# Whole banks gathered before their readout, and a gate unit moved from the first pair of experts to the last

## The chip, the cores and the metric

The kernel runs on one core of a Trainium2 chip. The metric is the device time of one execution in microseconds, the median of the runs shown; a profiled execution gives the trace.

## What is computed

Two blocks of a language model run one after the other on 512 tokens of 1024 features, in float32. The change touches the mixture of experts that ends each of the two layers of the second block:

```
def expert_choice_moe(x, router_w, w1, w3, w2):
    cap = EC_CAPACITY_FACTOR * s // N_EXPERTS
    aff = jax.nn.softmax(jnp.einsum('bsd,de->bse', x, router_w).astype(jnp.float32), axis=-1)
    gates, idx = lax.top_k(aff.transpose(0, 2, 1), cap)
    xg = jax.vmap(lambda xb, ib: xb[ib])(x, idx)
    hid = jax.nn.silu(jnp.einsum('becd,edf->becf', xg, w1)) * jnp.einsum('becd,edf->becf', xg, w3)
    ye = jnp.einsum('becf,efd->becd', hid, w2) * gates[..., None].astype(x.dtype)
    return jax.vmap(lambda yb, ib: jnp.zeros((s, d), x.dtype).at[ib.reshape(-1)].add(yb.reshape(-1, d)))(ye, idx)
...
        ffn = expert_choice_moe(x, router_w[i], w1[i], w3[i], w2[i])
        ple = jax.nn.sigmoid(x @ ple_gate_w[i] + ple_gate_b[i]) * (p[i] @ ple_w[i])
        x = layer_norm(DEEPNORM_ALPHA * x + ffn + ple, ln2_g[i], ln2_b[i])
```

There are 16 experts, each takes 64 of the 512 tokens, and w1, w3 and w2 of an expert are 1024x1024 each. `ple` is a gated side input; its 1024 features are worked out in eight units of 128.

## The kernel before

`experts` (called by `moe`, once in each layer: the first and the second stage below) goes through eight pairs of experts, `pi` 0 to 7. The weights of a pair are 24 chunks of 128x2048 floats (1024 KB). SyncE issues all their loads in one order, into a ring of eight buffers (`cyc`: three of the pool `wr`, five of `r1`); a load waits until the chunk eight places before it has been used. A unit's gate weights (`unit`, 512 KB) take one place in the same ring, and its second weights `pw` (128x256) have a buffer of their own.

A pair runs like this. For each half of the hidden features, `pair_product` multiplies w1 into `a1` and w3 into `a3`, eight chunks a half: two experts side by side, 64 columns each, the chunks as the moving operand. Between the first half and the second TensorE scatters the result of the pair before (`scatter`, `sc`), works out a unit if the table `units_a` names one, and transposes the selection `og` (`ot`). After the second half it finishes an open unit (`rest`, the transposes `pt`), turns the hidden values (`hidden`, `ht`), gathers the tokens of the next two pairs if `pi` is 1, 3 or 5 (`gather`), works out a unit if `units_b` names one, and multiplies w2 (`y`, eight chunks). Units 0 and 1 of the eight are worked out before the stage. For pair 0 the gather is split: two banks before the first product, two between the products of w1 and w3 with the first and the second half of the inputs (`kc`).

`gather` makes the 1024 features of the chosen tokens, eight tiles of 128x256, two tiles to a bank of PSUM: eight matmuls a tile with the one-hot matrix `OH`, then a scale and shift into `xg`, on VectorE for the bank's first tile and on ScalarE for its second (L1664 to L1671). `ple_unit` splits the gate weights into a high part (`whi`, ScalarE, L218) and a low part (`wlo`, VectorE or every fourth time GpSimd, L221), does 24 matmuls into `pg` and 6 into `pv`, and takes tanh of `pg`.

TensorE's order in `experts` is kept as it is written (`keep_order`); the other engines and SyncE follow a scheduler. At the last pair `ef.close()` gives back the memory that the units use, and in the second layer the gain and bias of the final norm (`lng`, `lnb`, 512 KB each) are loaded into it.

Of the kernel before, what the change touches and what calls it, by code (L numbers as in the profile page):

```python
# [14 lines left out]
AF = mybir.ActivationFunctionType  # L15
OP = mybir.AluOpType
# [129 lines left out]
class K:  # L146
# [1473 lines left out]
    def experts(self, l, xhl, aff, slT, slot, g, b, st, ef, r1, early):  # L1620
        nc, I, C = self.nc, self.ins, self.C
        x = self.xtok
        w1, w3, w2 = I["w1_2"][l], I["w3_2"][l], I["w2_2"][l]
        with ExitStack() as es:
# [25 lines left out]
            def one_hot(grp):  # L1650
                OH = p.tile([128, 4, 4, 64], F32R, name="OH")
                nc.vector.tensor_tensor(OH, slT[:, :, 4 * grp:4 * grp + 4, None].to_broadcast([128, 4, 4, 64]),
                                        slot[:, None, None, :].to_broadcast([128, 4, 4, 64]), op=OP.is_equal)
                return OH

            def gather(xg, OH, k2s):

                for k2 in k2s:
                    ps = pp.tile([128, 2, 256], F32, name="ga", tag=("t", "y", "sc", "y")[k2])
                    for kk in range(2):  # L1660
                        k = 2 * k2 + kk
                        for t in range(4):
                            for a in range(2):
                                nc.tensor.matmul(ps[:, kk], xhl[a][:, t, 128 * k:128 * k + 128],  # L1664
                                                 OH[:, t].rearrange("p e s -> p (e s)"),
                                                 start=t == 0 and a == 0, stop=t == 3 and a == 1)
                        if kk:
                            nc.scalar.activation(xg[:, k], ps[:, kk], AF.Identity, scale=g[:, k:k + 1], bias=b[:, k:k + 1])
                        else:
                            nc.vector.tensor_scalar(xg[:, k], ps[:, kk], g[:, k:k + 1], b[:, k:k + 1],  # L1670
                                                    op0=OP.mult, op1=OP.add)  # L1671

            def hidden(th, half, hT):
                ps = pp.tile([128, 4, 128], F32, name="ht", tag="t")
# [4 lines left out]
            def scatter(oT, ys, halves, last=False):  # L1679
                for half in halves:  # L1680
                    yh, yl = ys[half]
                    for t in range(4):
                        ps = pp.tile([128, T], F32, name="sc", tag=("y", "sc")[t % 2] if not last else "sc")
                        ts_ = slice(128 * t, 128 * t + 128)
                        nc.tensor.matmul(ps, oT[:, ts_], yh, start=True, stop=False)  # L1685
                        nc.tensor.matmul(ps, oT[:, ts_], yl, start=False, stop=True)  # L1686
                        xs = x[:, t, 512 * half:512 * half + 512]
                        nc.vector.tensor_add(xs, xs, ps)  # L1688
                        if last:
                            self.ln_stats(p, st[:, t], x[:, t], half)  # L1690
                            if half and l == 0:
                                self.ln_norm(p, st[:, t], x[:, t])
# [9 lines left out]
            def rest(u):  # L1702
                if u:
                    next(u)

            first = len(nc.cur_bb.bb.instructions)
            OH = one_hot(0)
            xg = p.tile([128, 8, 256], F32, name="xg")
            gather(xg, OH, range(2))
            left = u = None  # L1710
            units_a, units_b = {0: 2, 3: 5}, {0: 3, 2: 4, 4: 6, 6: 7}
            for pi in range(8):
                grp, pr = divmod(pi, 2)
                e0 = 2 * pi

                og = p.tile([128, 4, 2, 64], F32, name="og")
                nc.gpsimd.tensor_mul(og, OH[:, :, 2 * pr:2 * pr + 2], aff[:, :, e0:e0 + 2, None].to_broadcast([128, 4, 2, 64]))  # L1717
                if pr and pi < 7:
                    OH = one_hot(grp + 1)
                hT = p.tile([128, 8, 128], F32, name="hT")  # L1720
                ths = []
                for half in range(2):
                    xa = lambda a, k: xg[:, k, 128 * pr + 64 * a:128 * pr + 64 * a + 64]
                    a1, a3 = [pp.tile([128, T], F32, name="a", tag="a") for _ in range(2)]
                    for kc in range(2):
                        if pi == half == 0 and kc == 1:
                            gather(xg, OH, range(2, 4))
                        pair_product(a1, w1, e0, xa, half, kc)
                        if pi == half == kc == 0:
                            for h in range(2):  # L1730
                                G, Bb = self.ln_half(p, l, h, "yh", "yl")
                                for t in range(4):
                                    xs = x[:, t, 512 * h:512 * h + 512]
                                    nc.gpsimd.tensor_mul(xs, xs, G)
                                    nc.gpsimd.tensor_add(xs, xs, Bb)
                                for m in range(2) if h == 0 else ():
                                    xs = x[:, :, 128 * m:128 * m + 128]
                                    nc.gpsimd.tensor_add(xs, xs, early[m].rearrange("p (t f) -> p t f", t=4))
                        pair_product(a3, w3, e0, xa, half, kc)
                    th = p.tile([128, T], F32, name="th", bufs=2)  # L1740
                    nc.scalar.activation(th, a1, AF.Tanh, scale=0.5)  # L1741
                    nc.vector.scalar_tensor_tensor(th, th, 1.0, a1, op0=OP.add, op1=OP.mult)  # L1742
                    nc.vector.tensor_mul(th, th, a3)
                    ths.append(th)

                    rest(u)
                    u = None
                    if half == 0:
                        if left:
                            scatter(*left, range(2))  # L1750
                        if pi in units_a:
                            u = unit(units_a[pi])
                        ps = pp.tile([128, T], F32, name="ot", tag="t")
                        for t in range(4):
                            nc.tensor.transpose(ps[:, 128 * t:128 * t + 128], og[:, t].rearrange("p e s -> p (e s)"), C["ident"])
                        gate = p.tile([128, 1], F32, name="gate", bufs=2)
                        ogT = p.tile([128, T], F32, name="ogT", tag="og")
                        nc.scalar.activation(ogT, ps, AF.Copy, scale=0.5, accum_out=gate)
                        oT = p.tile([128, T], F32R, name="oT", bufs=2)
                        nc.vector.tensor_scalar(oT, ogT, 0.0, None, op0=OP.is_gt)  # L1760
                        if pi == 7:
                            ef.close()
                            if l == 1:
                                G, Bb = self.ln_load(es.enter_context(self.pool("lng", 1, side="right")), l, "ln2")
                    else:
                        hidden(ths[0], 0, hT)
                        if pr and pi < 7:
                            xg = p.tile([128, 8, 256], F32, name="xg")
                            gather(xg, OH, range(4))
                        if pi in units_b:  # L1770
                            u = unit(units_b[pi])
                        hidden(th, 1, hT)
                if pi == 7:
                    self.exp_ln_table()
                ys = []
                for half in range(2):
                    y = pp.tile([128, T], F32, name="y", tag="y")
                    for kc in range(2):
                        pair_product(y, w2, e0, lambda a, k: hT[:, k, 64 * a:64 * a + 64], half, kc)
                        if pi == 7 and half and kc == 0:  # L1780
                            scatter(oT, ys, range(1), True)
                    yh = p.tile([128, T], F32R, name="yh", bufs=2)
                    yl = p.tile([128, T], F32R, name="yl", bufs=2)
                    nc.scalar.activation(yh, y, AF.Copy, scale=gate)  # L1784
                    nc.vector.scalar_tensor_tensor(yl, y, gate, yh, op0=OP.mult, op1=OP.subtract)  # L1785
                    ys.append((yh, yl))
                left = oT, ys
            scatter(*left, range(1, 2), True)
            self.keep_order(first)
            if l == 1:  # L1790
# [111 lines left out]
```

## Time and profile before

| what | value |
| --- | --- |
| three runs, median (lowest to highest) | 3506.03 us (3505.88 to 3511.51) |
| the profiled execution, its own time | 3509.84 us |
| its span, first to last instruction | 3508.0 us |
| mean granted TensorE clock | 0.971 |
| busy share of the span: PE, PEld, DVE, ACT, POOL | 94%, 61%, 45%, 31%, 15% |
| HBM over the span | 166 GB/s |

PE is TensorE's matmuls, PEld its weight loads, DVE is VectorE, ACT ScalarE, POOL GpSimd, SP SyncE. The busy share of an engine is a mean over stages that differ: the middle of a row of slices tells more than the share. A DMA share is the mean busy share of 16 DMA engines.

### The profile page before, as it was taken

What the parts mean: (1) busy time and instruction counts of PE and PEld (TensorE: products, weight loads), DVE (VectorE), ACT (ScalarE), POOL (GpSimd) and SP (SyncE); (2) the same over time, 40 slices, a digit from 0 to 9 for tenths busy, and PEclk for the clock granted to TensorE, in tenths of its full rate; (3) what the DMA queues carried; (4) which work ended last, traced back from release to release, by engine and by line L of the source; (5) the groups of instructions that cost most, each with busy time, mean ns of one, the idle gap of its engine ahead of it and who ended that gap; (6) DMA issues with size and microseconds to landing.
All of it is one profiled execution on the core that took longest, in us unless ns stands there. A gap on an engine that the chain in (4) does not pass through costs nothing. (4 is left out here: it accounts for less than half of the span.)

```text
span 3508.0 us, 37612 instructions
## 1 busy us (share of the span) xinstructions
PE 3305.6 (94%) x15018; PEld 2155.8 (61%) x15018; DVE 1582.8 (45%) x2527; ACT 1070.3 (31%) x1933; POOL 510.7 (15%) x357
## 2 busy tenths in 40 slices
PE   8999999999999999999989889999997999999996
PEld 6666578888766657888866765344435657444342
DVE  6555463444555546344457753122216775211213
ACT  4333333223333333322355432011013553111011
POOL 2012121001101212100230423000003103100001
PEclk9999999999999999999999989999998998999998
DMA  5101132234210113233220225999992013899997
GB/s 183 48 25 61 37 110 81 96 96 137 75 60 13 61 36 106 77 96 96 90 86 3 72 102 227 407 412 386 417 421 85 28 43 113 366 408 378 421 407 301
DMA packets 223583, 584.85 MB, mean 167 GB/s; under 512 B 17584, under 2 KB 160304, under 8 KB 173232
## 3 DMA queue, kind: packets, MB, share of 16 engines
q1 hardware_dynamic: 222976, 581.66, 43.9%
q8 instruction: 118, 1.93, 0.2%
q10 hardware_dynamic: 432, 0.79, 0.1%
q14 instruction: 57, 0.47, 0.0%
HBM read 580.30 MB, written 2.10 MB: 166 GB/s over the span
## 5 line engine op out<-in xcount | busy, mean ns | idle before, releaser
L218 ACT CAST whi<-w 128x1024 fp32r<-128x1024 f32 (+1 forms) x312 | 311.2, 1003 | 731.7 <-PE mm L228 498.8
L1647 PE MATMUL a<-w,xg 128*64 128x512 f32 x2048 | 481.4, 600 | 42.2 <-DMA w<-in_w_dram 42.2
L227 PE MATMUL mm<-h,whi 128*128 128x512 f32 x1056 | 417.9, 396 | 4.8 <-ACT whi L218 4.1
L229 PE MATMUL mm<-h,wlo 128*128 128x512 f32 x1056 | 415.0, 394 | 0.4 <-POOL wlo L221 0.3
L228 PE MATMUL mm<-l,whi 128*128 128x512 f32 x1056 | 412.0, 390 | 0.0
L221 DVE TENSOR_TENSOR wlo<-w,whi 128x1024 fp32r<-128x1024 f32 (+1 forms) x237 | 306.4, 1297 | 233.8 <-ACT whi L218 232.5
L1647 PEld LDWEIGHTS a<-w,xg 128*64 128x64 f32 x2048 | 158.5, 138 | 348.6 <-issue 252.8
L221 POOL TENSOR_TENSOR wlo<-w,whi 128x1024 fp32r<-128x1024 f32 x75 | 166.2, 2218 | 642.4 <-ACT whi L218 445.0
L1647 PE MATMUL y<-w,hT 128*64 128x512 f32 x1024 | 226.3, 594 | 3.3 <-DMA w<-in_w_dram 3.3
L227 PEld LDWEIGHTS mm<-h,whi 128*128 128x128 f32 x1056 | 199.3, 189 | 48.1 <-ACT whi L218 5.3
L229 PEld LDWEIGHTS mm<-h,wlo 128*128 128x128 f32 x1056 | 199.0, 188 | 47.2 <-DVE wlo L221 1.0
L228 PEld LDWEIGHTS mm<-l,whi 128*128 128x128 f32 x1056 | 199.0, 188 | 44.7 <-issue 0.7
L602 DVE TENSOR_REDUCE mx<-s 128x1 f32<-128x128 f32 x192 | 93.3, 489 | 192.6 <-PE s L601 191.7
L1742 DVE SCALAR_TENSOR_TENSOR th<-th,a 128x512 f32<-128x512 f32 x32 | 22.0, 688 | 317.5 <-ACT th L1741 317.5
L1647 PEld LDWEIGHTS y<-w,hT 128*64 128x64 f32 x1024 | 72.4, 137 | 144.8 <-issue 136.3
L604 ACT ACTIVATE P<-s,mx 128x128 f32<-128x128 f32 x192 | 100.9, 527 | 174.5 <-DVE mx L602 162.3
L948 POOL TENSOR_TENSOR u<-u 128x512 f32<-128x512 f32 x64 | 66.6, 1040 | 521.4 <-ACT E L947 275.5
L1717 POOL TENSOR_TENSOR og<-OH,aff 128x512 f32<-128x512 f32 x16 | 16.8, 1047 | 764.2 <-DVE oT L1760 747.6
L1785 DVE SCALAR_TENSOR_TENSOR yl<-y,gate,yh 128x512 fp32r<-128x512 f32 x32 | 24.0, 751 | 223.3 <-ACT yh L1784 223.3
L959 DVE TENSOR_TENSOR y<-mm,r 128x512 f32<-128x512 f32 x64 | 44.2, 691 | 160.8 <-PE mm L229 160.8
L1741 ACT ACTIVATE th<-a 128x512 f32<-128x512 f32 x32 | 19.1, 597 | 319.8 <-PE a L1647 319.8
L621 PEld LDWEIGHTS pt<-c_ident,P 128*128 128x128 f32 x480 | 54.8, 145 | 73.1 <-issue 63.9
(584 smaller groups left out, 6414.2 us busy)
## 6 DMA issues: line engine op xcount, KB each, us to landing
w<-in_w_dram SPq DMA_DIRECT2D x384, 1024.0 KB, 12.6
w<-in_w_in_dram SPq DMA_DIRECT2D x32, 1024.0 KB, 5.3
w<-in_w_up_dram SPq DMA_DIRECT2D x32, 1024.0 KB, 5.5
w<-in_w_down_dram SPq DMA_DIRECT2D x32, 1024.0 KB, 5.1
w<-in_w_out_dram SPq DMA_DIRECT2D x8, 1024.0 KB, 5.2
w<-in_w_o_dram SPq DMA_DIRECT2D x8, 1024.0 KB, 4.7
w<-in_ple_gate_w_dram SPq DMA_DIRECT2D x16, 512.0 KB, 4.9
w<-in_w_in_even_dram SPq DMA_DIRECT2D x7, 1024.0 KB, 5.4
```

The costliest lines, as they stand in the source:

```text
L218: nc.scalar.copy(h, view)
L221: e.tensor_sub(l, view, h)
L227: mm(ps, wh, xh, start=first, stop=False)
L228: mm(ps, wh, xl, start=False, stop=False)
L229: mm(ps, wl, xh, start=False, stop=last)
L602: nc.vector.tensor_reduce(mx[:, i:i + 1], s[:, :n], axis=X, op=OP.max, negate=True)
L604: nc.scalar.activation(pv, s[:, :n], AF.Exp, bias=mx[:, i:i + 1], accum_out=sums[:, i:i + 1])
L621: nc.tensor.transpose(ps[:, (i - k) * 128:(i - k + 1) * 128], P[h][0][i][:, k * 128:(k + 1) * 128], C["ident"])
L948: nc.gpsimd.tensor_mul(u, u, u)
L959: nc.vector.tensor_mul(y, ps, r2)
L1647: nc.tensor.matmul(ps[64 * a:64 * a + 64], lhs(a, 4 * kc + k), cw[a][:, k], start=kc == 0 and k == 0, stop=kc == 1 and k == 3)
L1785: nc.vector.scalar_tensor_tensor(yl, y, gate, yh, op0=OP.mult, op1=OP.subtract)
```

## The change

In `gather` both tiles of a bank are multiplied first, then read out, one by VectorE and one by ScalarE. The tables of the units change: pair 0 had units 2 and 3, pair 2 unit 4, pair 3 unit 5, pair 4 unit 6 and pair 6 unit 7; now pairs 0, 2, 3, 4, 6 and 7 have one each, 2 to 7 in order. Since pair 7 now has a unit, `ef.close()` and the load of the last norm's gain and bias come after the loop.

```
                         for t in range(4):
                             for a in range(2):
                                 nc.tensor.matmul(ps[:, kk], xhl[a][:, t, 128 * k:128 * k + 128], ...
-                        if kk:
-                            nc.scalar.activation(xg[:, k], ps[:, kk], AF.Identity, scale=g[:, k:k + 1], bias=b[:, k:k + 1])
-                        else:
-                            nc.vector.tensor_scalar(xg[:, k], ps[:, kk], g[:, k:k + 1], b[:, k:k + 1],
-                                                    op0=OP.mult, op1=OP.add)
+                    k = 2 * k2
+                    nc.vector.tensor_scalar(xg[:, k], ps[:, 0], g[:, k:k + 1], b[:, k:k + 1], op0=OP.mult, op1=OP.add)
+                    nc.scalar.activation(xg[:, k + 1], ps[:, 1], AF.Identity, scale=g[:, k + 1:k + 2], bias=b[:, k + 1:k + 2])
...
-            units_a, units_b = {0: 2, 3: 5}, {0: 3, 2: 4, 4: 6, 6: 7}
+            units_a, units_b = {3: 4, 7: 7}, {0: 2, 2: 3, 4: 5, 6: 6}
...
-                        if pi == 7:
-                            ef.close()
-                            if l == 1:
-                                G, Bb = self.ln_load(es.enter_context(self.pool("lng", 1, side="right")), l, "ln2")
...
                 left = oT, ys
+            ef.close()
+            if l == 1:
+                G, Bb = self.ln_load(es.enter_context(self.pool("lng", 1, side="right")), l, "ln2")
             scatter(*left, range(1, 2), True)
```

On ScalarE, in pair 0 of a stage, before: `xg<-ga` are the readouts of the gather's second tiles, `whi` is the split of unit 2's gate weights.

```order
L1668 ACTIVATE xg<-ga,cols 128x256 [waits DVE_49,PE_49] x2
L218 CAST whi<-w 128x1024 [waits DMAHW0_49,Activation_49]
L1668 ACTIVATE xg<-ga,cols 128x256 [waits DVE_49,PE_49] x2
L1741 ACTIVATE th<-a 128x512 [waits PE_49]
L1607 ACTIVATE pz<-pg,cols 128x512 [waits PE_49,Pool_49]
```

The same place now:

```order
L1669 ACTIVATE xg<-ga,cols 128x256 [waits DVE_49] x4
L1739 ACTIVATE th<-a 128x512 [waits PE_49]
L1756 ACTIVATE ogT,gate<-ot 128x512 [waits PE_49,Pool_49]
L1739 ACTIVATE th<-a 128x512 [waits PE_49]
L218 CAST whi<-w 128x1024 [waits DMAHW0_49,Activation_49]
```

The split of unit 2 stands behind all four readouts and both halves' tanh, and a readout waits for VectorE alone, whose own waits for TensorE. VectorE's `wlo` moved in the same way.

On TensorE, after the second gather of pair 0 (`ga`) and the products that follow it, what was added ahead of the unit's matmuls (`pg`) there:

```order
 L1664 MATMUL ga<-OH,xkl 128x256
 L1647 MATMUL a<-w,xg 64x512 x16
+L1753 MATMUL ot<-c_ident,og 128x128 x4
+L1647 MATMUL a<-w,xg 64x512 x32
+L1674 MATMUL ht<-c_ident,th 128x128 x4
 L227 MATMUL pg<-xfh,whi 128x512
 L228 MATMUL pg<-xfl,whi 128x512
```

The second half's products now follow the first's with the four transposes `ot` between them, and the unit comes after. Inside the banks of a gather, the matmul that opens the second tile carries a wait for VectorE before and none now.

On SyncE, at the end of the second stage, before: the gate chunk of unit 7, which pair 6 uses, the norm's loads eight chunks behind it, then the last pair's 24 chunks.

```order
L1697 DMA w<-in_ple_gate_w_dram 128x1024
L1639 DMA w<-in_w_2_dram 128x2048 x8
L1378 DMA lng<-in_ln_g_dram 128x1024
L1378 DMA lnb<-in_ln_b_dram 128x1024
L1639 DMA w<-in_w_2_dram 128x2048 x24
```

And now, from unit 6's gate chunk on:

```order
L1695 DMA w<-in_ple_gate_w_dram 128x1024
L1639 DMA w<-in_w_2_dram 128x2048 x16
L1695 DMA w<-in_ple_gate_w_dram 128x1024
L1639 DMA w<-in_w_2_dram 128x2048 x8
L1378 DMA lng<-in_ln_g_dram 128x1024
L1378 DMA lnb<-in_ln_b_dram 128x1024
L1639 DMA w<-in_w_2_dram 128x2048 x8
```

Unit 7's chunk and the norm's loads moved into the last pair; eight chunks, those of w2, are left behind them.

## Rows read from the trace of the kernel before

**Rows 1.** The page's 40 slices of the span (87.7 us each), in tenths.
```profile
DMA  5101132234210113233220225999992013899997
```
**Rows 2.** Waits of PE, second stage: us in total, times, longest us.
```profile
PE a L1647 <- DMA w<-in_w_dram: 21.5, 19, 2.1
PE ga L1664 <- DVE xg L1670: 12.0, 16, 2.4
```
**Rows 3.** Windows: us; PE, PEld, DVE, ACT, POOL busy (x); PEclk, DMA share, GB/s.
```profile
2981.00:3036.00 55.00, 51.97 (x244) 28.16 (x242) 11.26 (x15) 8.46 (x14) 15.37 (x12) 0.94 0.82 331
3088.00:3102.00 14.00, 12.72 (x72) 6.57 (x73) 1.63 (x3) 2.41 (x5) 0.00 (x0) 1.00 0.84 334
...
3220.00:3232.00 12.00, 10.72 (x63) 5.95 (x63) 1.09 (x2) 1.82 (x4) 0.00 (x0) 1.00 0.42 160
3348.00:3358.00 10.00, 10.00 (x52) 4.14 (x53) 0.67 (x1) 1.73 (x3) 0.00 (x0) 1.00 0.76 298
2141.00:2200.00 59.00, 55.97 (x268) 29.42 (x266) 10.81 (x15) 9.15 (x15) 15.51 (x12) 0.97 0.87 351
2248.00:2262.00 14.00, 13.57 (x68) 5.50 (x70) 1.12 (x2) 1.73 (x3) 0.00 (x0) 1.00 0.83 331
2376.00:2390.00 14.00, 12.72 (x74) 6.83 (x74) 1.24 (x3) 2.81 (x5) 0.00 (x0) 1.00 0.51 200
...
2490.00:2530.00 40.00, 36.93 (x194) 18.52 (x196) 4.81 (x8) 4.70 (x8) 0.00 (x0) 1.00 1.00 412
```
**Rows 4.** Timeline of PE, pair 3, second stage: start, us, what [idle before <-releaser].
```profile
3214.66 0.27 PE L1664 MATMUL ga<-OH,xkl 128*128 128x256 f32 x1
3215.57 0.39 PE L1664 MATMUL ga<-OH,xkh 128*128 128x256 f32 x1 [0.64 <-DVE xg L1670]
3215.80 0.28 PE L1664 MATMUL ga<-OH,xkl 128*128 128x256 f32 x1
3215.91 0.28 PE L1664 MATMUL ga<-OH,xkh 128*128 128x256 f32 x1
...
3225.60 13.95 PE L1647 MATMUL y<-w,hT 128*64 128x512 f32 x64
```
**Rows 5.** Timeline of PE, pair 0, second stage.
```profile
2983.69 0.39 PE L1664 MATMUL ga<-OH,xkh 128*128 128x256 f32 x1
...
2987.30 0.38 PE L1664 MATMUL ga<-OH,xkh 128*128 128x256 f32 x1 [2.39 <-DVE xg L1670]
...
2993.17 7.89 PE L1647 MATMUL a<-w,xg 128*64 128x512 f32 x32
3000.99 0.50 PE L227 MATMUL pg<-xfh,whi 128*128 128x512 f32 x1
...
3007.93 0.60 PE L1755 MATMUL ot<-c_ident,og 128*128 128x128 f32 x4
```
**Rows 6.** Timeline of DVE, the same place.
```profile
2984.80 1.99 DVE L221 TENSOR_TENSOR wlo<-w,whi 128x1024 fp32r<-128x1024 f32 x1 [9.33 <-ACT whi L218]
```
**Rows 7.** The tile xg: ns min/median/max, first and last start.
```profile
L1670 DVE TENSOR_SCALAR xg<-ga,cols x32: 531/544/545, 2129.9 to 3347.2; 128x256 f32<-128x256 f32 x32
```
**Rows 8.** Timeline of PE, pair 7, second stage.
```profile
3448.68 15.01 PE L1647 MATMUL a<-w,xg 128*64 128x512 f32 x64
...
3465.12 4.50 PE L1647 MATMUL y<-w,hT 128*64 128x512 f32 x18
...
3478.53 0.50 PE L1685 MATMUL sc<-yh,oT 128*128 128x512 f32 x1
...
3481.30 3.65 PE L1647 MATMUL y<-w,hT 128*64 128x512 f32 x16
```
**Rows 9.** Windows, columns as in rows 3: behind the long stop; where TensorE waits for chunks.
```profile
2990.00:2991.00 1.00, 0.53 (x3) 0.23 (x2) 0.43 (x1) 0.00 (x0) 1.00 (x2) 0.50 1.04 434
...
3420.00:3430.00 10.00, 7.76 (x28) 2.05 (x24) 0.75 (x1) 0.69 (x1) 0.00 (x0) 0.83 1.01 421
```
**Rows 10.** Sum of the windows from 2640 to 2971 us, between the stages.
```profile
sum 331.00, PE 299.05 PEld 209.83 DVE 226.52 ACT 157.49 POOL 76.84; mean PE 37.38 PEld 26.23 DVE 28.31 ACT 19.69 POOL 9.60
```

## The prediction

> **What bounds the kernel now.** I read the slices of the span first [rows 1]: the DMA row holds nine tenths in two stretches, slices 26 to 30 and 36 to 39, and only there. These are the two expert stages (the MoE of each layer), near 2130 to 2640 us and 2970 to 3485 us, and only there does the change add, remove or rewrite work. The waits of TensorE inside the second stage come next [rows 2]: its products wait 19 times for a weight chunk, and its gather 16 times for VectorE's readout. So two things hold this stage, and the windows [rows 3] say which one when. With the weight stream running, the 16 DMA engines show a share of 1.01 at 421 GB/s [rows 9]; a chunk of 1024 KB (1.049 MB) takes 2.49 us. A stage needs 192 chunks and six half-size gate chunks; TensorE takes 13.95 us for eight [rows 4], 1.74 each, so it drains faster than DMA fills and then waits. But there are only eight buffers. Whenever TensorE does other work for long (gather, gate unit, scatter), the buffers fill, the queue has nothing to issue, and the share drops. **Time in which DMA is idle is the time that can be won; time in which TensorE waits for a chunk is not.** From rows 3, idle = length x (1 - share). Second stage: 55 x 0.18 = 9.9 us in pair 0, 14 x 0.16 = 2.2 in pair 1, 12 x 0.58 = 7.0 in pair 3, 10 x 0.24 = 2.4 in pair 5. First stage: 59 x 0.13 = 7.7 in pair 0, 14 x 0.17 = 2.4 in pair 1, 14 x 0.49 = 6.9 in pair 3, none in pair 5. Between any two of these TensorE waits for chunks, so each saving stays saved.
>
> **Part 1, the gather.** Now all 16 matmuls of a bank come before its two readouts, so the stop in the middle of each bank goes: VectorE's readout need not end before the second tile starts. The stop in [rows 4] runs from a start at 3214.66 to the next at 3215.57, 0.91 us; neighbours inside a half are 0.12 apart, so a stop costs 0.79. A gather of four banks loses 3.2 us with its stops and is otherwise unchanged. What it is worth depends on DMA idle there: pair 3 keeps 7.0 - 3.2 = 3.8 idle, saving 3.2; pairs 1 and 5 had less idle than 3.2, so 2.2 and 2.4 are saved and the rest becomes waiting for chunks. First stage: 2.4, 3.2 and 0.
>
> The readouts themselves are 0.54 us on VectorE [rows 7] and about as much on ScalarE. In the new order ScalarE's waits for VectorE's, so a bank is read some 1.2 us after its last matmul, while the next bank's 16 matmuls take 16 x 0.12 = 1.9: hidden. Only in pair 0 do products follow the gather at once. They start with tile k = 0 and use 0.87 us a tile (3.49 for four), so the last bank's tiles are wanted 1.7 and 2.6 us after it ends, and are ready after 0.7 and 1.3. I cost this at nothing. The Trainium skill (PSUM — Partial Sum Buffer, Terms) speaks against the new form: no two engines may access one bank at once, two reads included, so the two readouts of a full bank can't overlap. By it they run one after the other; if 1.2 us were exposed after each of pair 0's two gathers, the sum would be 2 x 2 x 1.2 = 4.8 us worse.
>
> **Part 2, the start of a stage.** All eight buffers are full before the first product, and the stream restarts when that product frees two. The first two banks stand ahead of it, with two of the 16 stops [rows 2], so the stream restarts 2 x 0.8 = 1.6 us earlier in each stage.
>
> **Part 3, pair 0.** The second half of that gather had a longer stop, 2.39 us [rows 5]: VectorE's readout stood behind the low part of unit 2's weights, 1.99 us on VectorE [rows 6], which in turn waited for the unit's gate chunk. Unit 2 is now in half 1, behind the gather on ScalarE and VectorE, so this goes with the stops. Right behind the long stop the granted clock is 0.50 of full speed [rows 9], the 1.2 GHz level, for the rest of the gather and the start of the products of 2993.17, whose 32 records take 7.89 us against 6.98 at 2.4 GHz. The 32 matmuls take 32 x 0.12 = 3.9 us instead of the 9.5 between 2983.7 and 2993.17. Then the unit leaves: 3007.93 - 3000.99 = 6.9 us of TensorE between the products of half 0 and half 1. Between two releases of buffers there were thus 9.5 + 3.5 = 13.0 us, then 6.9 + 0.5 + 3.5 = 10.9; now 7.4 and 4.0 (3.5 being one product of two chunks). Four chunks, 10 us, are issued ahead of the first gap over the 3.5 us before it; they last 10 - 3.5 = 6.5 us into 7.4, so 0.9 idle is left and none in the second gap. Saved: 9.9 - 0.9 = 9.0 in the second stage, 7.7 - 0.9 = 6.8 in the first. Unit 3, moved to pair 2, takes the place that unit 4 had, and units 5 and 4 the same way, so pairs 1 to 6 keep their load of TensorE.
>
> The small loads stand in SyncE's queue and block it: the one of a unit's 128x256 weights waits for VectorE's split of the one before. They keep their distance to the gate chunks, behind the eighth chunk after one. There the next chunk needs a buffer that a product frees only after the unit, so the block costs nothing, unless the unit before were to end later than that product. Every fourth split stays on GpSimd, for another unit; nothing waits for it.
>
> **Part 4, pair 7.** Unit 7 now adds 6.9 us and a transpose of 0.4 after the last pair's first half. There TensorE waits for chunks, by [rows 8], 15.01 - 13.95 = 1.1 us in the products of the second half, and from 3465.12 to the scatter at 3478.53 another 13.4 - 10.5 (six chunks of w2) = 2.9; the unit may use these 4.0, and 3.3 are left over. Against this, what moves behind the last pair's first chunks no longer delays them: the gate chunk (1.25 us), and in the second stage also the two final norm loads (1 MB, 2.5 us). Second stage: 3.75 - 3.3 = 0.4 saved; first: 3.3 - 1.25 = 2.0 lost. On SyncE the norm loads wait for unit 7's last matmul, now as before, when it stood in pair 6; the last eight chunks now stand behind them, but those need buffers freed 4.0 us after that matmul, so the wait is covered. They are used by the final norm some 30 us later.
>
> **Sum.** Second stage 1.6 + 9.0 + 2.2 + 3.2 + 2.4 + 0.4 = 18.8; first 1.6 + 6.8 + 2.4 + 3.2 - 2.0 = 12.0; together 30.8. The profiled execution took 3509.8, so 3479.0; it stands 3.8 above the median of the three runs, 3506.0, so the forecast is **3475 us**.
>
> **Rivals.** (a) *The tail pays for the unit in full.* If the last pair has no waits to fill, because unit 7's chunk or its split on VectorE comes late, 7.3 is lost in each stage: 7.7 more in the second and 5.3 in the first, 3488. For it: only 4.0 us of waits are there to fill [rows 8]. Against: unit 5 sat in the same place in pair 3 without a visible stop. (b) *The middle moves.* The scheduler also reorders the second layer's attention, between the stages, where TensorE is idle 32 of 331 us [rows 10]. A third of that either way is 11 us: 3464 or 3486. Against: the same work in nearly the same order. (c) *Slower, by the clock.* TensorE now waits for chunks where it used to work, and in a stretch of such waits the granted clock was 0.83 [rows 9]. If the clock fell at each last wait, scatter, unit and transposes (16 matmuls at the pace of the unit's 30, 3.7, then 6.9 + 0.5 and the first product's 3.5, together 15 us) would take 30, against some 18 us of chunks issued by then (seven to eight buffers): 12 us idle per pair. From three such pairs of sixteen the gain is gone; with four it is 3475 + 48 = 3523. The Trainium skill (TensorE: Matmul & The Clock Gate, HAM oscillation) describes this pattern, DMA waits that throttle each next group. Against, by the rows: no wait for a chunk exceeds 2.1 us [rows 2], and the dips that show lie where DMA was at 1.01 anyway. (d) *The change does not do what it says*: a stop stays inside the banks. The new order has none on TensorE; the gather's part would be missing, 3475 + 13 + 3 = 3491.
>
> **Numbers.** Forecast 0.72, (a) 0.12, (b) 0.09, of which a little reaches no change, (c) 0.03, (d) 0.04. Low end: all idle of rows 3 goes, another 9.3, with a little of (b): 3464. High end: (a), with (d) and a little of (b) reached: 3493. A measurement of this kernel tells 0.2%, 7 us, from no change. Faster by more 0.92, within it 0.05, slower 0.03.
>
> **What would show it.** Right: no waits of the gather for VectorE on TensorE but at its start; the DMA share near 1 through pair 0 and in pairs 1 and 5, about 4 us idle left in pair 3; granted clock 1.0 around the second gather; the last product of each stage 12 to 19 us earlier against its first matmul. Wrong: the DMA share back below 0.9 in pairs 2, 4 or 7, a dip of the clock followed by it, or a last pair whose products never wait for a chunk and end over 40 us after its first half.

## The result and the profile after

Four runs of the changed kernel have a median of 3472.11 us (3471.57 to 3472.57), beside 3505.95 us for the kernel before on the same chip; the ratio is 0.9901, 95% interval 0.9884 to 0.9918. The forecast was 3475.0. The profiled execution took 3472.18 us, its span is 3470.4.

The two spans differ by 37.6 us. To see where, each stage is measured from the start of its first gather matmul to the start of its last matmul with w2. These two moments are the first start in the row of the tile `ga` and the last start in the row of `y`. Of the kernel before, one stage after the other (busy ns min/median/max, first and last start in us):

```profile
L1664 PE MATMUL ga<-OH,xkh x128: 278/282/582, 2128.6 to 2505.2; 128*128 128x256 f32 x128
L1647 PE MATMUL y<-w,hT x512: 592/592/644, 2187.1 to 2638.2; 128*64 128x512 f32 x171
L1664 PE MATMUL ga<-OH,xkh x128: 278/282/581, 2970.8 to 3348.6; 128*128 128x256 f32 x128
L1647 PE MATMUL y<-w,hT x512: 592/592/644, 3030.7 to 3484.4; 128*64 128x512 f32 x171
```

The same rows of the changed kernel:

```profile
L1664 PE MATMUL ga<-OH,xkh x128: 278/281/386, 2125.9 to 2481.1; 128*128 128x256 f32 x128
L1647 PE MATMUL y<-w,hT x512: 592/592/643, 2170.3 to 2621.3; 128*64 128x512 f32 x171
L1664 PE MATMUL ga<-OH,xkh x128: 277/283/385, 2951.8 to 3308.0; 128*128 128x256 f32 x128
L1647 PE MATMUL y<-w,hT x512: 592/592/643, 2996.2 to 3446.7; 128*64 128x512 f32 x171
```

| stretch | before | after | difference | forecast |
| --- | --- | --- | --- | --- |
| ahead of the first stage | 2128.6 | 2125.9 | -2.7 | 0 |
| first stage | 509.6 | 495.4 | -14.2 | -12.0 |
| between the stages | 332.6 | 330.5 | -2.1 | 0 |
| second stage | 513.6 | 494.9 | -18.7 | -18.8 |
| behind the last w2 matmul | 23.6 | 23.7 | +0.1 | 0 |

So nearly all of the gain lies in the two stages, as forecast. Their DMA row has changed little to the eye, since the slices are 87 us long; the clock row has no digit below 9 inside either stage (slices 25 to 30 and 35 to 39; the 31st and the 40th hold the ends and what follows them). From the page of the changed kernel:

```profile
PEclk9999999999999999999999989999998998999998
DMA  5101132334210112232220116999993113899997
```

The waits of TensorE in the second stage (us in total, times, longest; the first row of the list; the next has 1.1 us) show part of the swap that the argument needed. The 16 waits of the gather for VectorE's readout [rows 2], 12.0 us, are gone; the products' waits for chunks have grown from 19 to 24, from 21.5 us to 25.4, and none is longer than 1.3 us. Two more chunk waits before, of the products with w2 and 1.7 us together, are gone too.

```profile
PE a L1647 <- DMA w<-in_w_dram: 25.4, 24, 1.3
```

The windows answer to [rows 3] and [rows 9] (columns as there; PEclk, DMA share and GB/s stand last). In order: pair 0 behind its second gather, the gather of pair 1, the half and the gather of pair 3, the gather of pair 5, a stretch of waits for chunks, and the half of pair 7 in the first stage.

```profile
2965.00:2975.00 10.00, 10.00 (x57) 4.60 (x57) 2.46 (x4) 2.10 (x4) 10.00 (x9) 1.00 0.93 372
3050.00:3060.00 10.00, 10.00 (x78) 8.41 (x78) 2.18 (x4) 3.15 (x6) 0.00 (x0) 1.00 1.01 416
3165.00:3175.00 10.00, 10.00 (x50) 3.32 (x48) 0.67 (x1) 0.60 (x1) 0.55 (x1) 1.00 0.88 342
3185.00:3195.00 10.00, 10.00 (x56) 4.41 (x57) 0.90 (x3) 2.31 (x4) 0.00 (x0) 1.00 0.70 247
3300.00:3310.00 10.00, 10.00 (x79) 9.02 (x80) 2.87 (x5) 3.33 (x6) 0.00 (x0) 1.00 1.02 424
3385.00:3395.00 10.00, 7.35 (x36) 2.41 (x34) 0.00 (x0) 0.00 (x0) 0.00 (x0) 1.00 1.01 419
...
2590.00:2600.00 10.00, 10.00 (x50) 3.43 (x48) 0.39 (x1) 0.33 (x1) 0.00 (x0) 1.00 0.88 351
```

Idle DMA time, again length times (1 - share): pair 0 has 0.7 us left of 9.9, pair 1 none of 2.2, pair 3 at its gather 3.0 of 7.0, pair 5 none of 2.4. The 1.2 us at the half of pair 3 stood there before as well (a share of 0.74 from 3200 to 3205 us, 1.3 us). One place is new: 1.2 us at the half of pair 7 in the first stage, where unit 7 now stands.

The whole stages agree with these places. Here they are from their first gather matmul to their last w2 matmul, before and then after:

```profile
2128.60:2638.20 509.60, 473.45 (x2212) 215.70 (x2212) 103.64 (x160) 59.49 (x102) 36.47 (x28) 1.00 0.96 393
2970.80:3484.40 513.60, 476.77 (x2212) 216.37 (x2212) 104.87 (x161) 59.50 (x102) 34.12 (x27) 0.99 0.94 386
```

```profile
2125.90:2621.30 495.40, 466.67 (x2210) 211.83 (x2212) 102.74 (x160) 59.46 (x103) 35.54 (x28) 1.00 0.98 405
2951.80:3446.70 494.90, 467.23 (x2210) 212.10 (x2212) 103.97 (x161) 59.41 (x102) 33.16 (x27) 1.00 0.97 400
```

Length times GB/s is the same within 0.2%, so the bytes are the same. Cut into windows of 10 us, with the idle part of each added up (a share above 1 taken as 1), idle DMA fell from 28.3 to 14.3 us in the first stage and from 38.3 to 20.6 in the second. That is 14.0 and 17.7 us, where the stages got 14.2 and 18.7 shorter.

In pair 0, TensorE goes from the gather into the products and from there into the second half without a stop (start, us, what). The same stretch before is [rows 5].

```profile
2966.65 0.27 PE L1664 MATMUL ga<-OH,xkl 128*128 128x256 f32 x1
2966.85 7.09 PE L1647 MATMUL a<-w,xg 128*64 128x512 f32 x32
2973.87 0.66 PE L1753 MATMUL ot<-c_ident,og 128*128 128x128 f32 x4
2974.45 13.95 PE L1647 MATMUL a<-w,xg 128*64 128x512 f32 x64
```

### The profile page after: what moved, and what is told of

Its sections match the earlier page's. It is cut to its first block, busy times and chain, and to the rows that moved or that the text cites. A ratio compares the mean times of both kernels' runs of the same rounds, so it can differ in the third digit from the quotient of the medians.

```text
span 3470.4 us, 37599 instructions
## 1 busy us (share of the span) xinstructions
PE 3286.3 (95%) x15018; PEld 2145.0 (62%) x15018; DVE 1581.5 (46%) x2527; ACT 1069.3 (31%) x1933; POOL 509.0 (15%) x357
## 5 line engine op out<-in xcount | busy, mean ns | idle before, releaser
L1715 POOL TENSOR_TENSOR og<-OH,aff 128x512 f32<-128x512 f32 x16 | 16.8, 1048 | 677.2 <-DVE oT L1758 660.6
```

## The experiments

Eleven more runs followed, four of them of kernels that had run already. The time of a run varies by more than the stages do: the kernel before alone gave 3501 to 3512 us. Much of that goes with TensorE's granted clock: on one chip the kernel before took 3500.87 us at a mean clock of 0.974 and 3512.41 us at 0.970. The table therefore sets the stages of each trace beside the medians. Differences under 5 us are read from the stages. What lies ahead of the first stage is not the edits' doing: the thirteen traces have TensorE's matmuls there in one and the same order, and the stretch still varies by 10 us.

| kernel | ahead | first stage | between | second stage | median, us | ratio to before (95%) |
| --- | --- | --- | --- | --- | --- | --- |
| before (first trace) | 2128.6 | 509.6 | 332.6 | 513.6 | 3505.95 | |
| before_again | 2129.3 | 509.9 | 332.4 | 512.1 | 3510.3 | 1.0002 (0.9991 to 1.0012) |
| the change (first trace) | 2125.9 | 495.4 | 330.5 | 494.9 | 3472.11 | 0.9901 (0.9884 to 0.9918) |
| after_again | 2124.7 | 495.8 | 330.2 | 493.7 | 3473.0 | 0.9908 (0.9894 to 0.9922) |
| gather_only | 2122.0 | 495.8 | 330.2 | 495.7 | 3470.45 | 0.9890 (0.9875 to 0.9904) |
| gather_only_again | 2122.3 | 495.4 | 330.5 | 495.7 | 3469.38 | 0.9903 (0.9889 to 0.9918) |
| units_only | 2126.0 | 506.4 | 330.4 | 506.6 | 3495.74 | 0.9958 (0.9944 to 0.9973) |
| no_unit7 | 2125.8 | 490.7 | 328.2 | 490.7 | 3463.47 | 0.9874 (0.9858 to 0.9891) |
| ring7 | 2121.6 | 505.2 | 330.8 | 505.2 | 3492.56 | 0.9952 (0.9936 to 0.9968) |
| split | 2130.8 | 495.6 | 330.4 | 492.6 | 3470.4 | 0.9892 (0.9873 to 0.9912) |
| two_in_2_6 | 2126.1 | 492.9 | 329.7 | 491.3 | 3467.28 | 0.9889 (0.9870 to 0.9909) |
| two_in_2_6_again | 2131.7 | 492.1 | 330.4 | 491.5 | 3467.97 | 0.9891 (0.9875 to 0.9908) |
| split_two_in_6 | 2126.2 | 493.4 | 328.4 | 492.3 | 3467.05 | 0.9887 (0.9868 to 0.9905) |

### The new gather alone

The kernel before with the rewritten `gather` and nothing else:

```
-                        if kk:
-                            nc.scalar.activation(xg[:, k], ps[:, kk], AF.Identity, scale=g[:, k:k + 1], bias=b[:, k:k + 1])
-                        else:
-                            nc.vector.tensor_scalar(xg[:, k], ps[:, kk], g[:, k:k + 1], b[:, k:k + 1],
-                                                    op0=OP.mult, op1=OP.add)
+                    k = 2 * k2
+                    nc.vector.tensor_scalar(xg[:, k], ps[:, 0], g[:, k:k + 1], b[:, k:k + 1], op0=OP.mult, op1=OP.add)
+                    nc.scalar.activation(xg[:, k + 1], ps[:, 1], AF.Identity, scale=g[:, k + 1:k + 2], bias=b[:, k + 1:k + 2])
```

> The kernel before with the new gather alone; the units stay where they were (two in pair 0). My theory, that only DMA's idle time can be won: the start of a stage gives 1.6 us each, the gathers of pairs 1, 3 and 5 give 2.5, 3.5 and 2.6 in the second stage and 2.5, 3.5 and 0 in the first, as the changed kernel's DMA idle shows, and pair 0 gives most of the 5.6 us by which its second gather gets shorter, though unit 2 stays: some 27 us faster than before in all (22 to 32), about 3479. Rival 1, the parts simply add and the gather is worth only its stops (3.2 at the start, 13.4 in the later gathers): 17 us faster, 3489. Rival 2, the long stop behind the split of unit 2's weights stays and holds the first products after the gather instead: 14 us faster at most, with TensorE's products of pair 0 waiting 4 us or more for VectorE.

The stages are 13.8 and 17.9 us shorter than in the first trace of before, 31.7 together, at the upper edge of my theory; rivals 1 and 2 are out. The median is 38.5 us under that of before in the same runs (3509.0), above my range; the two profiled executions differ beyond the stages by 6.6 us ahead of them and 2.4 between them. It is as fast as the whole change. Idle DMA, added up as above, fell by 12.4 and 16.8 us. The long stop is gone although unit 2 stayed: its `wlo` still stands ahead of VectorE's readouts of the second gather, but the matmuls of the second tile no longer wait for a readout, and the split is over before the gather is. VectorE of this kernel, pair 0 of the second stage:

```profile
2960.10 1.46 DVE L221 TENSOR_TENSOR wlo<-w,whi 128x1024 fp32r<-128x1024 f32 x1 [7.44 <-ACT whi L218]
2961.48 0.53 DVE L1668 TENSOR_SCALAR xg<-ga,cols 128x256 f32<-128x256 f32 x1
2963.16 0.55 DVE L1668 TENSOR_SCALAR xg<-ga,cols 128x256 f32<-128x256 f32 x1 [1.15 <-PE ga L1664]
```

TensorE, same place: the products start without a wait, and the second half only at 2977.53, behind unit 2.

```profile
2963.05 7.09 PE L1647 MATMUL a<-w,xg 128*64 128x512 f32 x32
...
2977.53 12.67 PE L1647 MATMUL a<-w,xg 128*64 128x512 f32 x58
```

What the unit costs there shows in the windows behind it: 1.1 + 2.1 = 3.2 us of idle DMA.

```profile
2970.00:2980.00 10.00, 10.00 (x48) 6.97 (x48) 2.14 (x4) 1.78 (x4) 3.65 (x4) 1.00 0.89 364
2980.00:2990.00 10.00, 10.00 (x48) 3.30 (x46) 3.14 (x3) 1.64 (x2) 0.00 (x0) 1.00 0.79 310
```

### The units alone

The changed kernel with the old gather (the diff above, turned round).

> The changed kernel with the old gather (VectorE reads the first tile out before the second is multiplied); the units and the norm loads as in the changed kernel. My theory: pair 0 loses a unit of 6.9 us and the long stop, some 9.4 us of its idle DMA in each stage, and the last pair pays 4.1 in the first and 5.3 in the second stage for unit 7, less the chunks that now stand behind its first ones (1.25 and 3.75): 11 to 17 us faster than before, about 3492. Together with the gather alone that is more than the 33.8 us of both, since both use the same idle DMA of pair 0. Rival 1, the parts add: 33.8 less what the gather alone gives, to 3 us. Rival 2, the units move is nothing or a loss, because the tail pays as much as pair 0 wins: within 5 us of before.

The median is 13.3 us under that of before in the same runs (3509.0), inside my range of 11 to 17; the stages are 3.2 and 7.0 shorter, 10.2 together, which is below it. The first stage is the miss: the theory's terms give it 9.4 - 4.1 + 1.25 = 6.5. Idle DMA, added up as above, fell by 3.5 and 6.8 us. Both rivals are out: the parts do not add (below), and the move is not nothing. In the second stage the waits of the gather are back, 16 of them, but none is longer than 0.7: the order of units and splits does remove the long stop too.

```profile
PE a L1647 <- DMA w<-in_w_dram: 23.4, 22, 2.0
PE ga L1664 <- DVE xg L1670: 10.3, 16, 0.7
```

The parts overlap. Taken from the first trace of before, the gather alone gives 31.7 us in the two stages and the units alone 10.2; both together give 32.9, not 41.9. The idle DMA of pairs 0, 1 and 3 that the new gather removes is still there in units_only:

```profile
2982.00:2992.00 10.00, 10.00 (x50) 3.45 (x48) 2.24 (x4) 1.43 (x4) 5.35 (x5) 1.00 0.75 270
3072.00:3082.00 10.00, 9.34 (x54) 5.30 (x56) 0.54 (x1) 1.61 (x3) 0.00 (x0) 1.00 0.78 302
3202.00:3212.00 10.00, 8.72 (x58) 5.86 (x59) 1.09 (x2) 2.17 (x4) 0.00 (x0) 1.00 0.45 187
```

### The price of unit 7 in the last pair

```
-            units_a, units_b = {3: 4, 7: 7}, {0: 2, 2: 3, 4: 5, 6: 6}
+            units_a, units_b = {3: 4}, {0: 2, 2: 3, 4: 5, 6: 6}
```

> The changed kernel without unit 7: one of eight features tiles of the gated side input is left out in both layers, its gate weights are not loaded. It prices unit 7 in the last pair. My theory, that the last pair is bound by chunks without a unit and by TensorE with it: the last pair (its first scatter matmul to that of its own result) returns from 38.5 to about 34.4 us in the first stage and from 39.7 to about 34.4 in the second, and up to 1.25 less each since no gate chunk is loaded: 9 to 12 us faster than the changed kernel, with TensorE's products of w2 waiting again for chunks. Rival, the tail pays the unit in full: 7.3 in each stage and more, 15 us faster or above, with no waits of those products for chunks. Second rival, the waits of the last pair cover the unit whole: 3 us or less.

This kernel leaves work out, so it gives a price and is not a candidate. The stages are 4.7 and 4.2 us shorter than with unit 7 (5.1 and 3.0 by the second trace of the change). In sum that is 8.9 and 8.1, just under the 9 to 12 that I expected and far from both rivals. The last pair is bound by chunks again without the unit, by the same waits as in [rows 8]:

```profile
3399.63 15.02 PE L1647 MATMUL a<-w,xg 128*64 128x512 f32 x64
...
3416.08 4.50 PE L1647 MATMUL y<-w,hT 128*64 128x512 f32 x18
3420.95 3.65 PE L1647 MATMUL y<-w,hT 128*64 128x512 f32 x16 [0.36 <-DMA w<-in_w_dram]
3425.91 3.65 PE L1647 MATMUL y<-w,hT 128*64 128x512 f32 x14 [1.31 <-DMA w<-in_w_dram]
```

With the unit, in the changed kernel, the products of the second half are at their full pace and no wait is listed. The 48 matmuls with w2 ahead of the scatter take 10.52 us in the first stage and 11.65 in the second:

```profile
2605.04 10.52 PE L1647 MATMUL y<-w,hT 128*64 128x512 f32 x48
...
3413.36 13.95 PE L1647 MATMUL a<-w,xg 128*64 128x512 f32 x64
...
3429.31 11.65 PE L1647 MATMUL y<-w,hT 128*64 128x512 f32 x48
```

The 1.1 us between them lie where the norm's loads stand in SyncE's queue, right ahead of the last eight chunks (start, us, what). That they are the cause is argued from this order; no run took them away alone.

```profile
3412.79 0.33 SPq L1378 DMA_DIRECT2D lng<-in_ln_g_dram  x1
3413.46 0.33 SPq L1378 DMA_DIRECT2D lnb<-in_ln_b_dram  x1
3417.03 11.10 SPq L1639 DMA_DIRECT2D w<-in_w_dram  x8
```

### One buffer less

```
-R1=5
+R1=4
```

> The changed kernel with a ring of seven buffers in place of eight. My theory, that what is left to win or lose is decided by how long eight buffers keep the DMA queue supplied while TensorE does other work: each long stretch loses up to one chunk time, 2.5 us, more: pair 3 twice, the half of pair 7, and the gathers of pairs 1 and 5, which now have 0.6 us or less to spare; 10 to 20 us slower than the changed kernel, some 16, with DMA idle per stage up from about 5 to 11 us. Rival, with the waits of the gather gone TensorE's own work bounds the stage, or the chunks come at their rate whatever the number of buffers: within 3 us of the changed kernel.

The stages are 9.8 and 10.3 us longer, 20.1 together (20.4 by the medians): slower than my point of 16, just past the top of the range, and far from the rival's 3. Idle DMA grows where TensorE stays away longest: at the half of pair 7 in the first stage it is 3.6 in place of 1.2, in pair 3 3.4 and 3.3 in place of 1.2 and 3.0.

```profile
2592.00:2602.00 10.00, 10.00 (x50) 3.62 (x50) 1.11 (x2) 0.69 (x2) 0.00 (x0) 1.00 0.64 240
3168.00:3178.00 10.00, 10.00 (x49) 6.25 (x49) 1.45 (x3) 1.78 (x4) 1.05 (x1) 1.00 0.66 267
3198.00:3208.00 10.00, 10.00 (x48) 3.31 (x46) 0.75 (x1) 1.51 (x3) 0.00 (x0) 1.00 0.67 233
```

TensorE's work is the same as in the changed kernel, so the stage is bound by the supply of chunks, and the buffers decide how long the queue stays busy. Idle DMA, added up as above, does not explain all of it: it grows by 8.3 us in the first stage but by only 5.1 in the second. There about one chunk more is moved inside the stage (length times GB/s gives 199.2 MB, 198.1 with eight buffers), 2.5 us by the prediction's 2.49 a chunk; what is left stays open.

### Other places for gather and units

The gather in two pieces:

```
                             xg = p.tile([128, 8, 256], F32, name="xg")
-                            gather(xg, OH, range(4))
+                            gather(xg, OH, range(2))
...
                             scatter(oT, ys, range(1), True)
+                    if pr and pi < 7 and half == 0:
+                        gather(xg, OH, range(2, 4))
```

> The changed kernel with the gathers of pairs 1, 3 and 5 cut in two: two banks where all four stood, two between the halves of the w2 product. My theory: the buffers fill in pair 3 because the unit and then four banks follow too closely; in two pieces of 3.9 us none outlasts them. The 3.0 us of idle DMA at the gather of pair 3 go, the 1.2 at its half stay: each stage 3 us shorter (492.4 and 491.9 by the trace, first gather matmul to the start of the last w2 matmul), the kernel 6 faster than the changed one, 3466. Rival, the gather in the middle of the w2 product only moves the stop there, since the queue is then as full as before: stages as in the changed kernel within 1 us.

A miss in part. The second stage is 2.3 us shorter (3 expected; 1.1 against the second trace of the change), the first 0.2 longer, as the rival had it. In the first stage the dip at the gather of pair 3 has gone (0.96), but the half of pair 7 now shows 2.7 us of idle in place of 1.2:

```profile
2366.00:2376.00 10.00, 10.00 (x62) 5.68 (x60) 1.84 (x3) 1.81 (x3) 0.00 (x0) 1.00 0.96 386
2596.00:2606.00 10.00, 10.00 (x50) 3.43 (x48) 0.57 (x1) 0.60 (x1) 0.00 (x0) 1.00 0.73 283
```

Why the first stage gives back what the second keeps stays open.

Two units each in the pairs without a gather:

```
-            units_a, units_b = {3: 4, 7: 7}, {0: 2, 2: 3, 4: 5, 6: 6}
+            units_a, units_b = {2: 3, 6: 6}, {0: 2, 2: 4, 4: 5, 6: 7}
```

> The changed kernel with the units elsewhere: pairs 2 and 6, which have no gather, take two each (3 and 4, 6 and 7), pairs 0 and 4 one, pairs 3 and 7 none. My theory: pair 3 has no idle DMA left (4.2 in the first stage and 4.5 in the second now) and the last pair goes back to 34.4 us (38.5 and 39.7 now); each unit at a half costs about 1.2 of idle, as that of pair 7 shows, and unit 7's chunk (1.25) and in the second stage perhaps the norm's loads (2.5) come ahead of the last pair's chunks again: 4.7 in the first stage and 3.7 to 6.2 in the second, some 8 to 10 us faster than the changed kernel, 3463. Rival, two units in a pair leave it the same idle as pair 0 had with two (7.1 against 4 in pair 0, by the kernel with the gather alone): 3 us lost in pairs 2 and 6 each, no faster than the changed kernel.

The stages are 2.5 and 3.6 us shorter than in the changed kernel. The sign is the theory's and the rival is out (at their halves pairs 2 and 6 lose 0.4 and 0.7 us in the second stage, by the rows below, and 1.3 and 1.2 in the first, not 3), but the size is 6.1 where I had named 8 to 10. Idle DMA, added up as above, fell by 3.2 and 3.4 us. I had added the longer last pair (4.1 and 5.3) to the idle time that goes; my reading is that in much of that window DMA was busy and TensorE behind it.

```profile
3096.00:3106.00 10.00, 10.00 (x50) 4.15 (x50) 2.67 (x4) 1.77 (x4) 1.05 (x1) 1.00 0.96 387
...
3346.00:3356.00 10.00, 10.00 (x50) 3.36 (x48) 1.09 (x2) 1.53 (x2) 0.00 (x0) 1.00 0.93 371
```

Both ideas in part (the split gather, and `{3: 4, 6: 6}, {0: 2, 2: 3, 4: 5, 6: 7}`):

> The split gather, and unit 7 moved from pair 7 to pair 6, which then has two. My theory: 3.0 of idle go in pair 3, the last pair goes back to 34.4 us, pair 6 gets about 1.2 of idle and the chunk of 1.25 ahead of the last pair: 4.7 shorter in the first stage and 3.3 to 5.8 in the second, some 9 us faster than the changed kernel, 3463. Rival, the last pair's cost is only moved to pair 6, which lacks TensorE time for two units: as fast as the split gather alone.

The stages are 2.0 and 2.6 shorter, half of the expected; that it is for the same reason is not shown. The kernel is no better than the one before it in this list.

### The same kernels once more

> The kernel before once more, for a second trace. It tells what of the difference between the two first traces is the change: the stages (first gather matmul to the start of the last w2 matmul) should again be 509.6 and 513.6 us, within 0.5. What lies ahead of the first stage (2128.6 before, 2125.9 with the change) and between the stages (332.6 and 330.5) the change doesn't touch by my theory: these should vary here by as much, 2 to 7 us. Rival, the reordered middle is truly 2.1 us shorter with the change: then it is again 332.6 here.

The first stage came out the same (509.9), the second 1.5 shorter (512.1), more than the 0.5 that I had allowed. The difference lies in the clock behind the long stop of pair 0: the first trace has 0.76 granted in this window and a DMA share of 0.42,

```profile
2990.00:3000.00 10.00, 9.36 (x39) 4.23 (x40) 1.23 (x2) 1.16 (x2) 5.32 (x5) 0.76 0.42 161
```

and the second trace, in its own, 0.90 and 0.59:

```profile
2990.00:3000.00 10.00, 9.36 (x47) 4.38 (x46) 1.23 (x2) 1.51 (x3) 6.13 (x5) 0.90 0.59 221
```

So 1.5 of the 18.7 us of the second stage are the depth of one dip in one execution. Between the stages the second trace has 332.4, where every edited kernel has 328.2 to 330.8: here the rival was right, those 2 us come with the edits. What lies ahead of the first stage varies without one: 2126.1 and 2131.7 for one and the same kernel, below; from 1060 to 1113 us, for one, the granted clock was 0.94 in the first of these and 0.87 in the second.

> The changed kernel once more, beside the two that follow on one chip. By its first trace its stages are 495.4 and 494.9 us; again within 0.5 by my theory, since a stage is its stream of chunks. The time varies by what lies ahead of the stages: 3468 to 3474.

The stages are 495.8 and 493.7; the second differs by 1.2, more than the 0.5 that I had allowed. The time was 3469.9 to 3477.4, up to 3.4 over my range.

> The kernel before with the new gather alone, once more. Its first trace has stages of 495.8 and 495.7 us, 1.2 more in sum than the changed kernel. My theory now: the move of the units is worth 1 us and can't be told from nothing; the median within 3 us of the changed kernel's here. Rival, what the first runs showed (1.7 faster than the changed kernel) is real and the move costs something between the stages or ahead of them.

The stages repeat (495.4 and 495.7), in sum 1.6 over after_again; the median is 3.6 under it. My 3 us was too narrow, but the sign contradicts the stages. In the two traces what lies ahead of them differs by 2.4 (2122.3 against 2124.7), with TensorE's matmuls there in the same order, and between the stages they differ by 0.3: no cost of the move shows in either place, where the rival put it. With both traces of each, moving the units is worth 0 in the first stage and 1.4 us in the second. By time the two can't be told apart: the intervals of the ratios, 0.9903 (0.9889 to 0.9918) and 0.9908 (0.9894 to 0.9922), lie on each other.

> Two units each in pairs 2 and 6, none in 3 and 7, once more. Its first trace has stages of 492.9 and 491.3 us, 6.1 less in sum than the changed kernel. My theory: that is real, the median here 4 to 8 us under the changed kernel's. Rival, the difference of the first medians (4.8) came with the chip or with what lies ahead: within 3 us.

The stages are again 492.1 and 491.5, in sum 5.9 under after_again, and the median 5.0 under it, as the theory had it. Of the forms that leave nothing out it has the shortest stages; by the median split_two_in_6 is level with it (3467.05 and 3467.28). It is 5.0 us under the changed kernel here and 4.8 by the first medians, which come from two chips. The intervals of the ratios overlap (0.9891, 0.9875 to 0.9908), so the lead over the changed kernel rests on the stages of four traces.

## Why the prediction held

**What bounds the stage.** Right, and shown: a buffer less costs 20 us with the same work on TensorE, and the change shortened the stages by 14.2 and 18.7 us while idle DMA fell by 14.0 and 17.7.

**Part 1, the gather.** Right. Pairs 1 and 5 have no idle DMA left, pair 3 has 3.0 us at its gather where 3.8 was forecast. The readouts do run one after the other, as the page in the Trainium skill (PSUM — Partial Sum Buffer, Terms) led one to expect of a bank, and as the wait written into the new order does by itself: ScalarE's last one starts when VectorE's ends. VectorE and ScalarE of the changed kernel behind the second gather of pair 0:

```profile
2966.96 0.55 DVE L1668 TENSOR_SCALAR xg<-ga,cols 128x256 f32<-128x256 f32 x1 [1.37 <-PE ga L1664]
```

```profile
2967.54 0.56 ACT L1669 ACTIVATE xg<-ga,cols 128x256 f32<-128x256 f32 x1 [1.35 <-DVE xg L1668]
```

But the products start at 2966.85, 0.2 us after the last gather matmul, and run their 32 at the full 7.09: nothing of 1.2 us a gather is exposed. Costing it at nothing was right for this use; the 4.8 us that the prediction set against it did not come.

**Part 2, the start.** Sized a little low. The first product comes 2955.81 - 2951.79 = 4.0 us after the first gather matmul, 5.9 before (2970.79 to 2976.68): 1.9 us in place of 1.6, since these two stops cost 0.94 each and not 0.79: the matmul behind a stop also takes 0.22 until the next one starts, and not 0.12.

**Part 3, pair 0.** Right as a sum: 0.7 us of idle are left in the second stage where 0.9 was forecast, and the clock is 1.00 throughout. What the text did not say is which edit does it. It gave the long stop to the unit's removal as much as to the gather. The runs show that either edit alone removes the long stop, and that the gather alone leaves 3.2 us of the 9.9 idle; beside the gather, only these are the unit's to win.

**Part 4, pair 7.** The price was about right, the credit in the second stage too high. Unit 7 with its chunk costs 4.7 and 4.2 us; less 1.25 for the chunk that is 3.4 and 3.0, where 3.3 was forecast (3.9 and 1.8 by the second trace of the change). Of the 3.75 us credited for what no longer stands ahead of the last pair's first chunks, 1.1 comes back as slower products with w2; the norm's loads as their cause are argued, as said above. It means that the units' move, which the sum took as part of a gain of 15.8 in the two pairs 0, is worth about 1 us after the tail is paid.

**The sum.** The stages gave 14.2 + 18.7 = 32.9 where 30.8 was forecast; with the second traces of both kernels it is 14.1 + 18.4. Between the stages 2.1 were gained where 0 was forecast. So the total held because it was added up from idle DMA, whichever edit empties it; the text gave no price for each edit alone, and its story of pair 0 would have set the units' move too high.

**The rivals.** (a) The tail does not pay in full: 7.3 and the chunk would have been 8.5 a stage, not 4.7 and 4.2. (b) The middle moved, by 2.1 us, a fifth of the 11 that I gave it; all edited kernels share this, and TensorE's attention matmuls come in another order there. That the order gains the 2 us is not shown. (c) No dip of the clock followed the new waits: the window from 3385 to 3395 us holds 7.35 us of work in 10, less than the 7.76 of [rows 9], and its clock is 1.00 where that one had 0.83. The pattern that the Trainium skill describes (TensorE: Matmul & The Clock Gate, HAM oscillation) did not set in in the changed kernel, whose longest waits for a chunk are 1.3 us in this stage and 1.4 in the first. That is not a matter of how long the waits are: with the same gather and the units in their old places the clock did fall, behind waits of 0.89 and 1.36 us (gather_only, second stage):

```profile
3380.00:3390.00 10.00, 7.75 (x28) 2.14 (x26) 0.75 (x1) 0.69 (x1) 0.00 (x0) 0.83 1.02 423
```

DMA was at 1.02 in that dip, so it cost no DMA time. That is what the prediction held against this rival; what decides whether a dip comes stays open.

(d) The stops are gone from the banks.

Of the signs that I named for a wrong forecast one showed: the DMA share fell below 0.9 in pair 7 of the first stage, to 0.88 for 10 us. It cost the 1.2 us that are part of the unit's price there.

## What to carry to other kernels

Where a stage is bound by a stream of loads into a ring of buffers, as here, the time in which DMA is idle is what can be won. So a window table of the DMA share told the gain of an edit on TensorE before it was made, to 2 us in 33, and two edits that empty the same idle time did not add. When a change has two parts, forecast each part alone: the sum here was right, while one of its parts turned out to be worth next to nothing. A matmul that waits for the readout of another tile in its own bank can be removed by order alone; here the new order alone was as fast as the new order with the moved units.

## What the runs showed that was not expected

- One buffer of eight is worth 20 us here. That is more than the idle time left with eight inside the streams (some 11 us, without the first 10 us of each stage and the end of the second), since a shorter ring opens gaps at the gathers of pairs 1 and 5 too (a share of 0.86 to 0.87 over 10 us), where there were none.
- The half clock behind the long stop of the kernel before is not the same in each execution: 0.76 and 0.90 over the same ten microseconds, with 1.5 us of the stage between them.
- With the expert stage alone edited, the stretch between the stages is 2 to 4 us shorter in each of the edited kernels. TensorE's matmuls come in another order there than before; that this is the cause is not shown.
- TensorE's matmuls ahead of the first stage come in the same order in every kernel, yet this stretch took 2121.6 to 2131.7 us, and the granted clock in it differs from execution to execution. A difference of a few microseconds between two medians need not be the edit's.
